# Moving gain multiplies, gate products and weight conversions between engines at the stage boundaries of a four-layer recurrent trunk

## The chip, the cores and the metric

The kernel runs on one core of a Trainium2 chip. The metric is the device time of one execution in microseconds (us); less is better. The engines are named as in the profile: PE (TensorE, matmuls) with its weight loads PEld, DVE (VectorE), ACT (ScalarE), POOL (GpSimd) and SP (SyncE, which issues the DMAs, in order).

## The reference

One inference step of a small trunk, in fp32: 1024 prompt positions and 8 x 8 sampled positions, model width 1024, FFN width 2816, 8 heads of 128.

```python
def conv_ffn(x, buf, w_in, cw, cb, w_out):
    gate, up = jnp.split(x @ w_in, 2, axis=-1)
    gc, new_buf = causal_dwconv(gate, buf, cw, cb)          # width 3, per column
    return (jax.nn.gelu(gc) * up) @ w_out, new_buf

for i in range(DEPTH):                                      # DEPTH = 2
    if i % 2 == 0:
        mix, h, cbuf = rglru_mixer(x, ...)                  # gated linear recurrence, 8 heads
    else:
        mix, S = hgrn2_mixer(x, ...)                        # below
    x = layer_norm(ALPHA * x + mix, ln_g[i, 0], ln_b[i, 0])
    f, fbuf = conv_ffn(x, ...)
    x = layer_norm(ALPHA * x + f, ln_g[i, 1], ln_b[i, 1])
```

`hgrn2_mixer` projects x to q, f, v and g, turns f into a forget gate, runs a chunked matrix-state recurrence per head, normalises the output `o` of each head and forms `o * silu(g)` before the output projection. The outputs are the new x, the recurrent states and the last rows of the convolutions.

## The kernel before, in words

The residual stream `z` stays on chip as nine row blocks m of 128 rows (the ninth has 64) by 1024 columns. Every matrix product is done in three reduced-precision products: each operand is split in a high and a low part (`xa`, `x` for activations, `wb`, `wx`, `wxf`, `wr` for weights), and the products are high*high, high*low, low*high. So three matmul lines always stand together: L298 to L300 (input projection of HGRN2), L606 to L608 (mixer output), L1144 to L1146 (FFN output).

**Weights.** A raw tile comes by DMA from SP's queue (L140, into `raw` or `rawf`). ACT casts the high part (L185 or L214), POOL subtracts it for the low part (L186 or L215) into one of three places `wb` and a few more. `convert` makes one tile if a place is free, `pump` issues loads and calls `convert`, `release` gives places back after a step. Which engine subtracts is in `run["lo"]`.

**FFN input.** `products` (L1045, tile `ps_f`) multiplies 2 x 2 blocks with seven products instead of eight. The weight combinations for them are made by POOL (L178, L180, L182), the activation combinations by `to_sums(mp)` for row blocks mp and mp + 4: PE transposes (L373), ACT copies (L393, L390), DVE and POOL adds (L391 to L400). `to_sums` uses parts of `z` as scratch. The product loops over i = 0..6, and for the first pair of columns over two column parts c outside of it.

**Layer norm.** `ln_pipeline` runs behind the matmuls that make a block: `resid` adds the product to z (L411), `nrm_a` takes the statistics (L421 on DVE, L422 to L424 on ACT), `nrm_b` scales (L429 to L434 on DVE, then the gain multiply L436 on POOL) and `nrm_c` adds the bias (L447 on DVE) and saves z to memory (L452). With `sums=True`, after each mixer, the blocks come in the order 8, 0, 4, 1, 5, 2, 6, 3, 7, and `to_sums` follows as pairs get done; what remains is put in `pend` and done within the next step's work.

**FFN output.** `prod` sums over the columns j of a group (six in the first) for one row block m and column half n in one PSUM bank (`ps_fo`). The operand of each j is split by `y_part` (ACT copy, DVE L1131). Banks come from a ring of four.

**HGRN2 recurrence.** Work of head h is cut into pieces that are run between the matmuls of projections. In a `period`, `gram` makes decayed Gram products by halving levels (L1394 on POOL, L1401 on ACT, L1404 on DVE, L1424 on PE, masked copies L1434), `kq_prep` and `pair_prep` scale keys and queries (L1472 to L1498), `gate_batch` applies the sigmoid to f and q of the next head and to g of the head before (L1334 to L1342), `g_mul` multiplies y by g (L1592), `f_chain_a` and `f_chain_b` make the logs and prefix sums of the next head's gate (L1351 to L1368), `gram_pairs` makes the last Gram level (L1451, masked copy L1452), `kt_small` transposes keys and makes `vb` (L1518 on POOL), `p_small` updates the state (L1532, L1538, L1543).

The tile pools add waits by data, so the order in which a function issues instructions is the order on each engine. Lines of the profile are those of the kernel before.

## Time and profile before

| | |
|---|---|
| median of 3 runs | 2645.24 us (2645.12 to 2646.01) |
| profiled execution | 2643.24 us, span 2641.5 us |
| granted TensorE clock, mean | 0.972 of full speed |
| PE busy | 2528.3 us, 96% of the span |
| DVE, ACT, POOL busy | 1566.3 (59%), 950.4 (36%), 1425.1 us (54%) |

The span is the time from the first to the last instruction; the rest of the execution lies around it. A row of the timeline has start, duration, engine, line, operation, output<-input and, in brackets, how long the engine sat idle before and what released it. Rows with `x4` are four instructions in a row. An instruction's duration includes the time that it waits for something below the level of semaphores, so the same product has different durations at different places.

### The profile page before, as it was taken

How to read it: one execution, taken by the hardware profiler on the slowest of the kernel's cores; microseconds unless marked ns; L12 is line 12 of the kernel's file. 1: busy time of each engine (PE TensorE's matmuls, PEld its weight loads, DVE VectorE, ACT ScalarE, POOL GpSimd, SP SyncE). 2: the span in 40 equal slices, each digit the busy share in tenths (PEclk: the TensorE clock that was granted, in tenths of full speed). 3: DMA queues.
4: the chain of work that ended last, by engine and by line, in shares of the span. 5: the costliest groups of instructions: out<-in, count | busy, mean ns of one | idle time of the engine just before them, and what ended most of it. 6: DMA issues, size and time to landing. Idle time of an engine off the chain costs nothing. (4 is left out here: it accounts for less than half of the span.)

```text
span 2641.5 us, 39929 instructions
## 1 busy us (share of the span) xinstructions
PE 2528.3 (96%) x16007; PEld 2332.4 (88%) x16007; DVE 1566.3 (59%) x2412; ACT 950.4 (36%) x1643; POOL 1425.1 (54%) x1169
## 2 busy tenths in 40 slices
PE   9999969999999999989999999999799999999997
PEld 9999869999998888779898988877699999988886
DVE  5986456565556333748858486875566565662327
ACT  4775233233334011334445353453333333330113
POOL 2443378888875112336445453635788888841214
PEclk9999989999999999999899999999899999999999
DMA  4115122222225322121111111123223222263111
GB/s 131 39 45 166 36 72 66 83 80 84 83 66 184 133 81 82 58 78 57 42 33 42 50 42 34 53 67 115 64 73 92 83 66 83 77 232 131 58 46 71
DMA packets 205840, 209.80 MB, mean 79 GB/s; under 512 B 13201, under 2 KB 167953, under 8 KB 205614
## 3 DMA queue, kind: packets, MB, share of 16 engines
q1 hardware_dynamic: 205654, 207.25, 24.4%
q8 instruction: 126, 2.06, 0.3%
q14 instruction: 60, 0.49, 0.1%
HBM read 159.61 MB, written 47.61 MB: 78 GB/s over the span
## 5 line engine op out<-in xcount | busy, mean ns | idle before, releaser
L215 POOL TENSOR_TENSOR wb<-raw,wb 128x1024 fp32r<-128x1024 f32 (+1 forms) x80 | 195.8, 2451 | 577.2 <-ACT wb L214 371.6
L1045 PE MATMUL ps_f<-xa,wb 128*128 128x288 f32 (+1 forms) x3072 | 406.9, 293 | 28.4 <-ACT wb L185 24.3
L1045 PEld LDWEIGHTS ps_f<-xa,wb 128*128 128x128 f32 x3072 | 398.9, 192 | 32.0 <-ACT wb L185 24.9
L1050 DVE TENSOR_TENSOR z<-z,ps_f 128x256 f32<-128x256 f32 (+2 forms) x550 | 196.2, 378 | 364.8 <-PE ps_f L1045 307.9
L1045 PE MATMUL ps_f<-x,wb 128*128 128x288 f32 (+1 forms) x2496 | 322.8, 289 | 0.0
L1045 PEld LDWEIGHTS ps_f<-x,wb 128*128 128x128 f32 x2496 | 318.1, 189 | 0.0
L298 PE MATMUL ps_in<-xa,wb 128*128 128x384 f32 (+3 forms) x912 | 307.4, 337 | 5.7 <-ACT wb L214 5.4
L300 PE MATMUL ps_in<-xa,wb 128*128 128x384 f32 (+3 forms) x912 | 300.5, 330 | 6.1 <-POOL wb L215 6.1
L299 PE MATMUL ps_in<-xa,wb 128*128 128x384 f32 (+3 forms) x912 | 300.6, 330 | 0.3 <-DVE xa L356 0.3
L411 DVE SCALAR_TENSOR_TENSOR z<-z,ps_fo 128x512 f32<-128x512 f32 x128 | 87.8, 686 | 285.8 <-PE ps_fo L1146 273.1
L186 POOL TENSOR_TENSOR wb<-rawf,wb 128x512 fp32r<-128x512 f32 x116 | 165.6, 1436 | 57.0 <-ACT wb L185 56.3
L186 POOL TENSOR_TENSOR wb<-raw,wb 128x512 fp32r<-128x512 f32 x116 | 160.5, 1391 | 58.3 <-ACT wb L185 48.8
L214 ACT CAST wb<-raw 128x1024 fp32r<-128x1024 f32 (+1 forms) x83 | 82.0, 987 | 301.4 <-issue 189.9
L1098 DVE SCALAR_TENSOR_TENSOR z<-z,ptf 128x1104 f32<-128x1104 f32 x88 | 182.0, 2069 | 1.6
L298 PEld LDWEIGHTS ps_in<-xa,wb 128*128 128x128 f32 x912 | 173.7, 190 | 8.4 <-ACT wb L214 5.7
L300 PEld LDWEIGHTS ps_in<-xa,wb 128*128 128x128 f32 x912 | 173.2, 190 | 7.5 <-POOL wb L215 6.8
L299 PEld LDWEIGHTS ps_in<-xa,wb 128*128 128x128 f32 x912 | 173.7, 190 | 1.4 <-DVE xa L356 0.7
L436 POOL TENSOR_TENSOR z<-z,gb 128x1024 f32<-128x1024 f32 (+2 forms) x36 | 101.6, 2822 | 107.7 <-DVE z L434 107.7
L1045 PE MATMUL ps_f<-xa,wxf 128*128 128x256 f32 (+1 forms) x1152 | 149.8, 288 | 0.1
L1045 PEld LDWEIGHTS ps_f<-xa,wxf 128*128 128x128 f32 x1152 | 146.6, 188 | 0.5 <-ACT z L1065 0.5
L185 ACT CAST wb<-rawf 128x512 fp32r<-128x512 f32 x116 | 71.0, 623 | 209.6 <-POOL rawf L182 76.0
L185 ACT CAST wb<-raw 128x512 fp32r<-128x512 f32 x116 | 70.2, 623 | 195.8 <-POOL raw L182 63.7
(493 smaller groups left out, 5816.7 us busy)
## 6 DMA issues: line engine op xcount, KB each, us to landing
raw<-in_ffn_w_in_dram SPq DMA_DIRECT2D x44, 512.0 KB
rawf<-in_ffn_w_in_dram SPq DMA_DIRECT2D x44, 512.0 KB
ysave<-z SPq DMA_DIRECT2D x44, 512.0 KB
raw<-in_hg_w_in_dram SPq DMA_DIRECT2D x32, 512.0 KB
xa<-ysave SPq DMA_DIRECT2D x28, 544.0 KB
zsave<-z SPq DMA_DIRECT2D x24, 512.0 KB
raw<-in_ffn_w_out_dram SPq DMA_DIRECT2D x24, 512.0 KB
z<-zsave SPq DMA_DIRECT2D x24, 512.0 KB
```

The costliest lines, as they stand in the source:

```text
L185: act.copy(w[:, 0], src)
L186: run["lo"].tensor_tensor(w[:, 1], src, w[:, 0], ALU.subtract)
L214: act.copy(w[:, 0, :n], raw[:, :n])
L215: run["lo"].tensor_tensor(w[:, 1, :n], raw[:, :n], w[:, 0, :n], ALU.subtract)
L298: pe.matmul(ps[:, :n], lhsT=wh, rhs=xh, start=(k == 0), stop=False)
L299: pe.matmul(ps[:, :n], lhsT=wh, rhs=xl, start=False, stop=False)
L300: pe.matmul(ps[:, :n], lhsT=wl, rhs=xh, start=False, stop=(k == KT - 1))
L411: dve.scalar_tensor_tensor(zz, zz, a, ps, ALU.mult, ALU.add, accum_out=stat[:, m, n:n + 1] if acc else None)
L436: eng.tensor_tensor(z[:r, m, c], z[:r, m, c], gb[:r, 0, c], ALU.mult)
L1045: pe.matmul(ps[:, :n], lhsT=l, rhs=r, start=(kk == 0 and i < 4 and l is wh and r is xh), stop=(kk == 3 and l is wl), skip_group_check=(i > ...
L1050: dve.tensor_tensor(d, s, pv(ps), ALU.add)
L1098: dve.scalar_tensor_tensor(c[:, :L], gs[:, i:i + L], w[:, i:i + 1], c[:, :L], ALU.mult, ALU.add)
```

## The change

Six edits:

1. In a norm with sums, the gain multiply of the last two row blocks (3 and 7) goes from POOL to DVE.
2. At the end of every norm but the last, the places of the weights that its matmuls used are released when the last matmuls have been issued, and `convert` is called before and after the last `nrm_b`. The low parts made there go to POOL after a mixer, and to DVE at the start of HGRN2 (three 128x1024 subtractions).
3. `to_sums(2)` runs within the norm instead of among the FFN's first products. `to_sums(3)` runs before product i = 5 instead of i = 4 of the first column part.
4. Pairs 0 to 3 of `to_sums` use blocks (0,4), (0,4), (1,8), (2,6) as scratch instead of their own.
5. In the first group of the FFN output, the products j = 0 to 3 of the first three row blocks run first, then j = 4 and 5 of each.
6. In the recurrence, the product of g with its sigmoid and the product of y with g go from POOL to DVE in the periods of heads 1 to 6; `vb` is made in a function of its own, ahead of these on POOL.

```diff
@@ def to_sums(mp)
-            s = [z[:, m, i * 512:(i + 1) * 512].rearrange("p (k t) -> p k t", t=n) for m in ms for i in range(2)]
+            s = [z[:, m, i * 512:(i + 1) * 512].rearrange("p (k t) -> p k t", t=n)
+                 for m in ((0, 4), (0, 4), (1, 8), (2, 6))[mp] for i in range(2)]
@@ def parts(m)
+        if m in run["dve"]:
+            return (dve, slice(0, D)),
         return (pool, slice(0, D)),
@@ def ln_pipeline(...)
+        run["dve"] = order[-2:] if sums else ()
...
             elif final != "out":
+                if i == NT:
+                    release(run["held"])
+                lo = run["lo"]
+                run["lo"] = pool if sums else dve
+                convert()
                 mid()
+                convert()
+                run["lo"] = lo
...
-            if final != "out" and 3 <= i < NT:
+            if final != "out" and 3 <= i < NT + sums:
                 turn(order[i - 3])
...
-            for m in order[NT - 3:]:
-                if not sums or m >= 4:
-                    pend.append(lambda m=m: turn(m))
+            for m in order[NT - 1 if sums else NT - 3:]:
+                pend.append(lambda m=m: turn(m))
@@ gates of the first pair
-                    fills = {(2, 0): [fill], (4, 0): [flush]}
+                    fills = {(5, 0): [flush]}
@@ first groups of the FFN output
+                        first = 3 if n == 0 and gi == 0 else 0
+                        banks = [sbank("ps_fo") for _ in range(first)]
+                        for m in range(first):
+                            prod_part(banks[m], m, grp, ws, range(4))
                         for m in range(NT):
-                            prod(m, n, grp, ws, gi == 0, False)
+                            if m < first:
+                                prod_part(banks[m], m, grp, ws, range(4, grp[1]))
+                                resid(m, n, banks[m], True)
+                            else:
+                                prod(m, n, grp, ws, gi == 0, False)
@@ def period(h)
-                fns.append(lambda: gate_batch([h + 1], [h - 1] if h else [], pool))
+                fns.append(lambda: vb_prep(h))
+                fns.append(lambda: gate_batch([h + 1], [h - 1] if h else []))
                 if h:
-                    fns.append(lambda: g_mul(h - 1, pool))
+                    fns.append(lambda: g_mul(h - 1))
```

`prod_part` is the loop over j of `prod` for a given range of j. Lines after an edit shift: L436 becomes L438, L447 L451, L391 L393, L394 L396, L429 to L434 L431 to L436, L1144 to L1146 become L1160 to L1162, L1045 L1057, L1342 L1366, L1592 L1618, L1336 L1360, L1452 L1476, L1518 L1544.

The first place is the end of a norm with sums, on DVE (`gb` holds gain and bias, `stat` the statistics, `ps_f` is the FFN product). Before:

```order
L434 TENSOR_SCALAR z<-z,stat 128x1024
L421 TENSOR_SCALAR stat<-stat 128x1
L447 TENSOR_TENSOR z<-z,gb 128x1024
L429 TENSOR_SCALAR stat<-stat 128x1
L430 SCALAR_TENSOR_TENSOR stat<-stat 128x1
L431 TENSOR_SCALAR stat<-stat 128x1
L432 TENSOR_TENSOR stat<-stat 128x1
L434 TENSOR_SCALAR z<-z,stat 128x1024
L447 TENSOR_TENSOR z<-z,gb 128x1024 x2
L1050 TENSOR_TENSOR z<-z,ps_f 128x256
```

And in the changed kernel, from the second L434 (now L436) on:

```order
L436 TENSOR_SCALAR z<-z,stat 128x1024
L438 TENSOR_TENSOR z<-z,gb 128x1024
L451 TENSOR_TENSOR z<-z,gb 128x1024
L396 TENSOR_TENSOR z<-ps_t,z 128x512
L397 TENSOR_TENSOR z<-z,ps_t 128x512
L393 TENSOR_TENSOR xa<-ps_t,xa 128x4x128
L399 TENSOR_TENSOR z<-ps_t,z 128x512
L402 TENSOR_TENSOR z<-ps_t,z 128x512
L393 TENSOR_TENSOR x_0_2500<-ps_t,x_0_2500 128x4x128
L393 TENSOR_TENSOR x_0_2504<-ps_t,x_0_2504 128x4x128
L451 TENSOR_TENSOR z<-z,gb 128x1024
L1062 TENSOR_TENSOR z<-z,ps_f 128x256
```

The gain multiply (L438) has come onto DVE, and a whole set of sums (L396 to L393) stands between the last two bias adds (L451).

The second place is PE at the end of the first tile of the FFN output, n = 0. Before, product j = 4 follows j = 3 and the next tile follows j = 5:

```order
L1144 MATMUL ps_fo<-wxf_2934,xa 128x512
L1145 MATMUL ps_fo<-wxf_2934,xa 128x512
L1146 MATMUL ps_fo<-wxf_2934,xa 128x512
L1144 MATMUL ps_fo<-wxf_2934,xa 128x512
L1145 MATMUL ps_fo<-wxf_2934,xa 128x512
L1146 MATMUL ps_fo<-wxf_2934,xa 128x512
L1144 MATMUL ps_fo<-wb_86,xa 128x512
```

In the changed kernel, from j = 3 of the first tile on:

```order
L1160 MATMUL ps_fo<-wb_84,xa 128x512
L1161 MATMUL ps_fo<-wb_84,xa 128x512
L1162 MATMUL ps_fo<-wb_84,xa 128x512
L1160 MATMUL ps_fo<-wb_86,xa 128x512
L1161 MATMUL ps_fo<-wb_86,xa 128x512
```

After j = 3 (weights `wb_84`) the next tile's j = 0 (`wb_86`) comes, and the products with `wxf` follow when three tiles have got that far.

The third place is DVE in a period of the recurrence, from `pair_prep` to the last masked copies (`A` is the Gram matrix, `mk` its mask, `y8h` holds y and g). Before:

```order
L1497 TENSOR_TENSOR z<-z 128x544
L1498 TENSOR_TENSOR z<-z,th_9712 128x544
L1336 TENSOR_TENSOR th_9711<-th_9711,z 128x1088
L1351 TENSOR_SCALAR z<-z,lbt 128x1088
L1352 TENSOR_SCALAR z<-z 128x1088
L1353 TENSOR_SCALAR z<-z 128x1088
L1357 TENSOR_SCALAR th_9712<-z 128x1088
L1358 TENSOR_SCALAR z<-z 128x1088
L1452 COPY_PREDICATED A<-mk,ps_g 128x4x128 x2
```

In the changed kernel:

```order
L1521 TENSOR_TENSOR z<-z 128x544
L1522 TENSOR_TENSOR z<-z,th_9718 128x544
L1360 TENSOR_TENSOR th_9717<-th_9717,z 128x1088
L1366 TENSOR_TENSOR y8h<-y8h,z 128x1088
L1618 TENSOR_TENSOR y8h<-y8h 128x1088
L1375 TENSOR_SCALAR th_9719<-th_9719,lbt 128x1088
L1376 TENSOR_SCALAR z<-th_9719 128x1088
L1377 TENSOR_SCALAR z<-th_9719 128x1088
L1381 TENSOR_SCALAR th_9718<-th_9719 128x1088
L1382 TENSOR_SCALAR th_9719<-th_9719 128x1088
L1476 COPY_PREDICATED A<-mk,ps_g 128x4x128 x2
```

The two gate products (L1366, L1618) stand ahead of the gate chain and of the masked copy.

More of the change, by code (lines that the diff above doesn't have):

```diff
@@ L106, in hawk_hgrn2_convffn_deepnorm_kernel @@
     steps = []
-    run = {"ch": CH, "dma": 0, "cvt": 0, "phase": -1, "n": 0, "lo": dve}
+    run = {"dve": (), "ch": CH, "dma": 0, "cvt": 0, "phase": -1, "n": 0, "lo": dve}
     blocks = []
@@ L263, in run_steps @@
                     assert convert(), "no place for weights"
-                fn([blocks[i].w[0] for i in ids])
                 held = run.setdefault("held", [])
                 held.extend(ids)
+                fn([blocks[i].w[0] for i in ids])
                 if not (keep and steps[run["n"] + 1][3]):
@@ L1133, in prod, with prod_part @@
         def prod(m, n, grp, ws, scaled, acc):
+            ps = sbank("ps_fo")
+            prod_part(ps, m, grp, ws, range(grp[1]))
+            resid(m, n, ps, scaled, acc)
+        def prod_part(ps, m, grp, ws, js):
             f0, nf, i0 = grp
-            ps = sbank("ps_fo")
-            for j in range(nf):
+            for j in js:
                 y = yv[i0 + j]
@@ L1150, in prod @@
                     pe.matmul(ps, lhsT=yt, rhs=wl, start=False, stop=b)
-            resid(m, n, ps, scaled, acc)
         def states(g):
@@ L1514, in kt_small, with vb_prep @@
         T.put(kd)
-        vb = T.get()
-        s["vb"] = vb
+    def vb_prep(h):
+        vb = G["T"].get()
+        hg[h]["vb"] = vb
         v8 = G["v"][:NS, NT - 1, (h % 2) * P:(h % 2 + 1) * P]
@@ L1734, in last_smalls @@
             run_all(lambda: gram(h, 5), *ysp(4)),
-            run_all(lambda: kt_small(h), lambda: rms_small(h - 1)),
+            run_all(lambda: kt_small(h), lambda: vb_prep(h), lambda: rms_small(h - 1)),
             run_all(lambda: pair(h), *ysp(5, 6)),
```

## The prediction

> **What bounds the kernel now.** I read four views: the page's head, TensorE's list of waits, the timeline of every engine around each long wait, and a table by stage for the granted clock. In a row of the list of waits stand: engine, tile, line, what it waited for: us in all, times, longest.
>
> ```profile
> PE 2528.3 (96%) x16007; PEld 2332.4 (88%) x16007; DVE 1566.3 (59%) x2412; ACT 950.4 (36%) x1643; POOL 1425.1 (54%) x1169
> PE ps_f L1045 <- ACT wb L185: 24.3, 2, 12.9
> PE ps_p L1532 <- DVE A L1452: 13.6, 6, 2.5
> PE ps_fo L1146 <- DVE xa L1131: 10.7, 4, 3.6
> PE ps_in L300 <- POOL wb L215: 6.1, 1, 6.1
> 1300.00:1730.00 430.00, 410.54 (x2657) 383.82 (x2656) 295.76 (x481) 182.50 (x286) 219.18 (x217) 0.94 0.15 43
> ```
>
> TensorE is busy for 2528.3 us of a span of 2641.5, so 113 us of idleness is nearly all that can be won, and the change adds or removes no matmul. The first four waits are 54.7 us of it, and each of them is a place that the change touches. The last row (start:end, length, busy us of PE, PEld, DVE, ACT and POOL, clock) adds a second prize: with a clock of 0.94, six heads of the recurrence lose about 0.06 x 430 = 26 us.
>
> **A. From a mixer's norm to the FFN (twice).**
>
> ```profile
> 352.30 1.22 DVE L447 TENSOR_TENSOR z<-z,gb 128x1024 f32<-128x1024 f32 x1
> 357.04 3.25 POOL L436 TENSOR_TENSOR z<-z,gb 128x1024 f32<-128x1024 f32 x1 [1.32 <-DVE z L434]
> 360.25 1.26 POOL L178 TENSOR_TENSOR raw<-raw 128x512 f32<-128x512 f32 x1
> 361.54 0.62 ACT L185 CAST wb<-raw 128x512 fp32r<-128x512 f32 x1 [7.32 <-POOL raw L178]
> 362.21 0.85 PE L1045 MATMUL ps_f<-xa,wb 128*128 128x288 f32 x2 [12.93 <-ACT wb L185]
> 363.03 1.44 SPq L140 DMA_DIRECT2D rawf<-in_ffn_w_in_dram  x2
> 369.34 0.69 DVE L394 TENSOR_TENSOR z<-ps_t,z 128x512 f32<-128x512 f32 x1 [1.72 <-ACT z L393]
> 375.39 0.69 DVE L391 TENSOR_TENSOR x<-ps_t,x 128x512 fp32r<-128x512 f32 x1 [0.31 <-ACT x L390]
> 379.85 0.60 ACT L393 COPY z<-ps_t 128x512 f32<-128x512 f32 x1
> 382.56 1.74 PE L1045 MATMUL ps_f<-xa,wb 128*128 128x256 f32 x4 [0.34 <-ACT xa L390]
> ```
>
> TensorE waits 12.93 us for the second weight tile of the FFN. Its preparation, POOL L178, stands behind POOL's gain multiply L436 of the last row block. The change moves the last two of these multiplies to VectorE and lets the conversions go ahead of them. A 128x1024 product takes VectorE 1.22 us by L447, so two cost 2.4 us there and free about 6.6 us on POOL; the weight is then ready near 356. But other things are late next. The sums of blocks 2 and 6 are now made inside the norm; by the rows at 369.34 and 375.39 one set takes 376.08 - 369.34 = 6.74 us of VectorE. On VectorE the gain multiply of block 3 starts where the first L447 stands now, at 352.30; adding the multiplies, both adds L447 and the small statistics, VectorE is free near 360.6 and done with the sums at 367.3. Only then comes the last add, until 368.5. SP's queue is in order: its zsave waits for that add, and the next rawf load, issued at 363.03 now, stands behind it and goes out near 368.7. Landing takes at most 5.7 us (rows in C), so ACT can convert it at 374.4; the last transposed sums (ACT L393) follow in ACT's queue, and from there the second column part starts 382.56 - 379.85 = 2.7 us later. With the conversion ahead and POOL's share I get 378.6 instead of 382.56: 4.0 us saved, not 12.9. The second boundary has the same rows 1509 us later. A = 2 x 4.0 = 8 us. Lower end 1 each (the load 3 us later still); upper end 12.93 - 6.74 = 6.2 each, where nothing but the sums replaces the wait.
>
> **B. First output tiles of the FFN (twice).**
>
> ```profile
> 2348.42 0.39 PE L1144 MATMUL ps_fo<-wb,xa 128*128 128x512 f32 x1
> 2356.53 0.79 PE L1146 MATMUL ps_fo<-wxf,xa 128*128 128x512 f32 x1 [3.56 <-DVE xa L1131]
> 2359.98 0.79 PE L1146 MATMUL ps_fo<-wxf,xa 128*128 128x512 f32 x1 [1.80 <-DVE xa L1131]
> 2353.12 6.94 DVE L1131 TENSOR_TENSOR xa<-xa 128x1024 fp32r<-128x1024 f32 x4
> 2369.50 0.69 DVE L411 SCALAR_TENSOR_TENSOR z<-z,ps_fo 128x512 f32<-128x512 f32 x1 [6.08 <-DMA z<-zsave]
> 2375.33 0.69 DVE L411 SCALAR_TENSOR_TENSOR z<-z,ps_fo 128x512 f32<-128x512 f32 x1
> 2379.52 0.69 DVE L411 SCALAR_TENSOR_TENSOR z<-z,ps_fo 128x512 f32<-128x512 f32 x1 [2.23 <-PE ps_fo L1146]
> ```
>
> The product j of a tile needs its split operand, which VectorE makes (L1131); j = 4 and 5 come late, at 2356.5 and 2360. The change runs j = 0 to 3 of three tiles first: 36 matmuls instead of 12 from 2348.42 on. Two whole tiles of 18 matmuls are read 2379.52 - 2375.33 = 4.19 us apart, 0.233 each, so TensorE works until 2356.8. It still waits 2.0 us for j = 5 at 2359.98, finishes the three tiles at 2363.0 and the fourth at 2367.2. Then four PSUM banks hold unread tiles. The first is read by L411 at 2369.50, after a reload of z that is queued behind other DMAs and does not depend on TensorE; so a new wait of 3.0 us arises, to 2370.2. The fifth tile ends at 2374.4, against 2379.4 now (L411 at 2379.52 waits for it): 5.0 us. After a wait of this length I allow 1.1 us for half clock (an estimate: five matmuls at twice 0.23). B = 2 x 3.9 = 8 us; ends 0 (all given back at the bank) and 5 each.
>
> **C. Start of the HGRN2 projection (once).**
>
> ```profile
> 1128.25 1.06 ACT L214 CAST wb<-raw 128x1024 fp32r<-128x1024 f32 x1
> 1129.36 0.79 PE L298 MATMUL ps_in<-xa,wb 128*128 128x512 f32 x1 [5.45 <-ACT wb L214]
> 1131.04 3.25 POOL L436 TENSOR_TENSOR z<-z,gb 128x1024 f32<-128x1024 f32 x1 [3.91 <-DVE z L434]
> 1136.64 0.79 PE L300 MATMUL ps_in<-xa,wb 128*128 128x512 f32 x1 [6.06 <-POOL wb L215]
> L215 DVE TENSOR_TENSOR wb<-raw,wb 128x1024 fp32r<-128x1024 f32 x3 | 3.7, 1219 | 0.2 <-ACT wb L214 0.2
> 1138.11 9.63 SPq L140 DMA_DIRECT2D raw<-in_hg_w_in_dram  x3
> 1143.80 1.05 ACT L214 CAST wb<-raw 128x1024 fp32r<-128x1024 f32 x1
> ```
>
> The first wait stays: the conversion L214 does not move. The second goes: the low part L215 stood behind L436 on POOL; on VectorE it takes 1.22 us, right after ACT at 1129.31, so L300 can start at 1130.6, when the two matmuls before it end. C = 6.06 - 0.1 = 6 us. The last POOL multiply starts some 1.2 us later, and ACT's third conversion now stands ahead of the first evacuation and waits for a load (1138.11 to 1143.80 at most, here issued near 1131); TensorE has 24 matmuls of the next tile to cover that. Ends 4.5 and 6.1.
>
> **D. The recurrence.** In six heads the two gate products (L1342, L1592) move from POOL to VectorE, ahead of the masked copy L1452 for which TensorE waits; L1518 runs earlier on POOL.
>
> ```profile
> 1379.19 2.82 POOL L215 TENSOR_TENSOR wb<-raw,wb 128x1024 fp32r<-128x1024 f32 x1
> 1381.98 2.94 POOL L1518 TENSOR_TENSOR z<-v,sm 64x1024 f32<-64x1024 f32 x1
> 1371.75 1.27 DVE L1482 TENSOR_TENSOR z<-z 128x1088 f32<-128x1088 f32 x1
> 1374.13 2.69 DVE L1497 TENSOR_TENSOR z<-z 128x544 f32<-128x544 f32 x1
> 1379.73 3.43 DVE L1336 TENSOR_TENSOR th<-th,z 128x1088 f32<-128x1088 f32 x1
> 1388.21 1.34 DVE L1452 COPY_PREDICATED A<-mk,ps_g 128x512 f32<-128x512 int32 x2
> 1388.99 1.16 PE L1532 MATMUL ps_p<-v,z 128*128 128x128 f32 x8 [2.14 <-DVE A L1452]
> 1437.60 0.70 DVE L1498 TENSOR_TENSOR th<-th,z 128x544 f32<-128x544 f32 x1
> 1453.19 3.45 PE L1543 MATMUL ps_p<-z 64*128 64x512 f32 x4
> 1458.19 0.58 PE L1630 MATMUL ps_v<-wb,xa 128*128 128x256 f32 x1 [0.50 <-DVE gb L1538]
> ```
>
> A 128x1088 product takes VectorE 1.27 us with POOL idle, and L1336 of the same size takes 3.43 beside POOL L215: it ends 1.2 us after the POOL instruction ends (1382.01, then 1383.16). L1497, half the size, takes 2.69 instead of about 0.70. So VectorE sits through four POOL instructions in turn before L1452: L1342, L1592, L215, L1518. The Trainium skill, page "SBUF — State Buffer", section "Who interferes with whom", says why: VectorE and GpSimd share a pair of ports under an exclusive lock, and a VectorE instruction with two SBUF inputs blocks against a GpSimd instruction that reads SBUF. The rows agree, and by that rule a removed POOL product gives its time back to VectorE where it stood in the way, which would give the same sum.
>
> I walk VectorE's queue through the period at 1374 to 1389, in which it has no idle time. The low parts L215 held the port from 1379.8 to 1382.0, 2.2 us; L1518 from 1383.16 to 1384.92, 1.8; from there L1351 to L1358 took 3.3 until L1452. After the change L1518 runs some 17 us earlier, beside four L1404, and I charge its 1.8 there. So L1452 starts at 1374.1 + 1.8 + 1.4 (L1497, L1498) + 2.2 (L215, once) + 3.6 (three products) + 3.3 = 1386.4, not 1388.21: 1.8 us earlier, and TensorE's wait of 2.14 shrinks to 0.3. Six times 1.8 is D = 11 us. The lower end is 12 x 1.27 = 15 us lost (products added, nothing given back). The upper end is 13.6 + 26 = 39 us, with the waits gone and the clock full throughout.
>
> I count nothing for the clock. L1543 takes 3.45 us after the wait at 1452 where full speed would take about half, so the wait does cost clock. But when TensorE comes sooner it meets the next link, L1630 behind DVE L1538, which moves by only 1.8 us; the idle time moves there. The Trainium skill, page "TensorE: Matmul & The Clock Gate", Part 1, has the clock fall after about 3.4 us of idling. By that alone these 2.2 us waits would cost no clock; the row at 1453 speaks against it.
>
> **Sum.** 8 + 8 + 6 + 11 = 33 us. The profiled execution took 2643.24 us (span 2641.5 and 1.7 around it): 2610. The median of the runs is 2645.24, 2.0 higher: 2612. About 0.2% (5.3 us) can be told from no change.
>
> **Rivals.**
> - Clock won too: with the 2.2 us waits gone, the half-clock stretches of the recurrence go. For: the stretches follow those waits. Against: L1538. Half of 26 us and the rest of the 13.6: D = 28, total 50, 2595.
> - Late loads and full banks: A and B give 1 each per place and D half. For: SP's order in A, the bank in B. 2 + 2 + 6 + 6 = 16: 2629.
> - Slower: every moved product meets a POOL instruction and takes 3.43 us like L1336, and VectorE's neighbours stay as slow. L1452 comes 2 x 3.43 = 6.9 us later in six periods, 41 us, less A, B, C (22): 2645 + 19 = 2664. It decides from 4.6 us a period (22 + 5.3 over six). Against: two of the four POOL instructions in the way are the ones removed.
> - No change: VectorE comes 3 to 4 us later per period and eats A, B, C: 2645.
>
> **How the numbers follow.** Forecast 0.47, clock won 0.20, late loads 0.19, no change 0.07, slower 0.07. So faster 0.86, same 0.07, slower 0.07. The likeliest is 2612. The range runs from 2590 (clock won, a little more) to 2634 (late loads with D at nothing is 2635); it leaves out about 2 in 10, above for the most part.
>
> **What would show it.** A: the wait of 12.93 becomes several below 4, the second column part starts near 378.6, the rawf load near 368.7. B: the waits for L1131 become one of about 2 us, and a new one of 3 us for PSUM behind L411 appears. C: no wait at L300. D: L1336 and the products near 1.2 us except one in each period, waits for the masked copy of 0.3 us. The prediction is wrong if those waits grow instead, if the clock from 1300 to 1730 leaves 0.94 by 0.02 or more, or if TensorE waits longer for weights after the norms.

## The result and the profile after

The changed kernel takes 2615.36 us (median of 4 runs, 2611.44 to 2616.62) against 2645.18 us of the kernel before on the same chip: a ratio of 0.9884, 95% interval 0.9867 to 0.9902, so about 30 us less. The profiled execution took 2615.03 us, its span 2613.3. The head of the page and rows from the list of TensorE's waits after the change (engine, tile, line, what it waited for: us in all, times, longest):

```profile
PE 2506.9 (96%) x16007; PEld 2317.7 (89%) x16007; DVE 1559.5 (60%) x2431; ACT 951.9 (36%) x1643; POOL 1378.8 (53%) x1150
PE ps_t L373 <- DVE z L451: 22.3, 4, 9.0
PE ps_v L1656 <- DVE gb L1564: 7.3, 3, 2.4
PE ps_f L1057 <- ACT z L395: 6.8, 2, 3.4
PE ps_kt L1536 <- DVE A L1464: 5.7, 7, 1.4
...
PE ps_fo L1160 <- DVE z L413: 4.1, 2, 3.0
...
PE ps_fo L1162 <- DVE xa L1143: 3.9, 2, 2.0
```

The four waits that led the list before are gone or smaller, and others stand in their places. The number of matmuls is the same, 16007. The span is 28.2 us shorter; 21.4 of that is TensorE's busy time (2528.3 to 2506.9) and only 6.8 is idle time. The same matmuls were done in less time: they ran at a higher clock. Where that shortens the kernel is to be read by stage. Of the 21.4 us, 13.1 lie in stage D of the table below, 6.8 in the two stages A, 2.5 in B and C, and the start has 1.0 more. In A the idle time grew (21.0 to 21.6 and 19.7 to 22.4 us), and the nine runs below that share A's code take 516.9 to 517.1 us for the first and 515.9 to 516.2 for the second, with 8.5 to 13.7 us lost to the clock: there another chain sets the length, and the clock does not. In D the length follows the clock, and that is the main reading of this case.

The stages are cut at landmarks on TensorE (the first L373 of the first mixer's norm, the first output product of each FFN, the first product of HGRN2's input, the first ps_g of the recurrence, the first L373 of the second mixer's norm, the last matmul). Their lengths, in us of the two profiles:

| stage | before | after | change | forecast |
|---|---|---|---|---|
| start, to the first norm's sums | 320.66 | 322.51 | +1.85 | 0 |
| A, first | 518.80 | 516.97 | -1.83 | -4.0 |
| B, first | 289.90 | 285.08 | -4.82 | -3.9 |
| C | 62.44 | 56.13 | -6.31 | -6.0 |
| D | 638.98 | 625.24 | -13.74 | -11 |
| A, second | 517.64 | 516.01 | -1.63 | -4.0 |
| B, second | 279.09 | 277.36 | -1.73 | -3.9 |

The start is not an effect of the change: in this execution the clock was halved from 11.8 to 15.2 us, in a part whose instructions are the same; runs below with the same start (e5, e1) stand at 320.7 there. Below stands stage D in one row each (start:end, length, busy us of PE, PEld, DVE, ACT, POOL, clock, DMA share, GB/s), of before, of after, and the row of after that answers to the last row of the prediction's first list:

```profile
1191.80:1830.78 638.98, 613.58 (x3793) 561.46 (x3793) 453.16 (x763) 277.26 (x446) 314.78 (x297) 0.95 0.18 53
...
1180.69:1805.93 625.24, 600.49 (x3793) 553.86 (x3793) 433.08 (x775) 277.80 (x446) 284.85 (x285) 0.98 0.18 54
1300.00:1730.00 430.00, 410.96 (x2704) 385.01 (x2703) 294.08 (x506) 195.33 (x305) 189.09 (x199) 0.97 0.15 42
```

Both have 3793 matmuls. TensorE's idle time in D is 25.4 us before (638.98 - 613.58) and 24.8 after; its busy time fell by 13.1. Summing (1 - clock) x length over 40 equal pieces of D gives 28.9 us lost to the clock before and 15.5 after. So the clock's 13.4 us are all of D but 0.3.

### The profile page after: what moved, and what is told of

Same layout as the page of the kernel before. It is cut to its first block, busy times and chain, and to the rows that moved or that the text cites. A ratio compares the mean times of both kernels' runs of the same rounds, so it can differ in the third digit from the quotient of the medians.

```text
span 2613.3 us, 39952 instructions
## 1 busy us (share of the span) xinstructions
PE 2506.9 (96%) x16007; PEld 2317.7 (89%) x16007; DVE 1559.5 (60%) x2431; ACT 951.9 (36%) x1643; POOL 1378.8 (53%) x1150
## 5 line engine op out<-in xcount | busy, mean ns | idle before, releaser
L215 POOL TENSOR_TENSOR wb<-raw,wb 128x1024 fp32r<-128x1024 f32 (+1 forms) x77 | 201.2, 2616 | 618.4 <-ACT wb L214 415.7
L1057 PE MATMUL ps_f<-xa,wb 128*128 128x288 f32 (+1 forms) x3072 | 399.7, 290 | 15.0 <-ACT z L395 6.8
L1057 PEld LDWEIGHTS ps_f<-xa,wb 128*128 128x128 f32 x3072 | 392.5, 189 | 18.1 <-ACT z L395 7.6
L1057 PE MATMUL ps_f<-x,wb 128*128 128x288 f32 (+1 forms) x2496 | 323.0, 289 | 2.4 <-POOL wb L186 1.3
L1057 PEld LDWEIGHTS ps_f<-x,wb 128*128 128x128 f32 x2496 | 318.1, 189 | 3.2 <-POOL wb L186 1.7
L300 PE MATMUL ps_in<-xa,wb 128*128 128x384 f32 (+3 forms) x912 | 299.7, 329 | 0.0
L413 DVE SCALAR_TENSOR_TENSOR z<-z,ps_fo 128x512 f32<-128x512 f32 x128 | 87.8, 686 | 279.0 <-PE ps_fo L1162 266.5
L300 PEld LDWEIGHTS ps_in<-xa,wb 128*128 128x128 f32 x912 | 172.4, 189 | 1.4 <-DVE wb L215 0.8
L1057 PE MATMUL ps_f<-xa,wxf 128*128 128x256 f32 (+1 forms) x1152 | 149.8, 288 | 2.7 <-ACT z L1077 2.7
L1057 PEld LDWEIGHTS ps_f<-xa,wxf 128*128 128x128 f32 x1152 | 146.6, 189 | 3.1 <-ACT z L1077 3.1
L438 POOL TENSOR_TENSOR z<-z,gb 128x1024 f32<-128x1024 f32 (+2 forms) x32 | 88.6, 2767 | 103.4 <-DVE z L436 103.4
```

The source lines that it names most:

```text
L215: run["lo"].tensor_tensor(w[:, 1, :n], raw[:, :n], w[:, 0, :n], ALU.subtract)
L300: pe.matmul(ps[:, :n], lhsT=wl, rhs=xh, start=False, stop=(k == KT - 1))
L413: dve.scalar_tensor_tensor(zz, zz, a, ps, ALU.mult, ALU.add, accum_out=stat[:, m, n:n + 1] if acc else None)
L438: eng.tensor_tensor(z[:r, m, c], z[:r, m, c], gb[:r, 0, c], ALU.mult)
L1057: pe.matmul(ps[:, :n], lhsT=l, rhs=r, start=(kk == 0 and i < 4 and l is wh and r is xh), stop=(kk == 3 and l is wl), skip_group_check=(i > ...
```

## The experiments

Every run is on a chip with the kernel before beside it (medians of 2645.2 to 2646.7 us), and each edit is against the changed kernel unless said otherwise. One table for all, with the stages as above (the second A and B after the bar); "clock" is the us lost to the clock in D, worked out as above.

| run | median (range) us | ratio, 95% | A | B | C | D | clock | A / B second |
|---|---|---|---|---|---|---|---|---|
| e1 products on POOL | 2626.08 (2625.11-2632.97) | 0.9929 (0.9915-0.9944) | 516.95 | 285.15 | 56.31 | 638.46 | 29.1 | 515.96 / 275.89 |
| e2 whole tiles | 2621.59 (2619.62-2622.67) | 0.9907 (0.9890-0.9923) | 517.10 | 289.27 | 57.29 | 623.60 | 13.7 | 515.96 / 279.59 |
| e3 low parts on POOL | 2612.98 (2611.71-2617.90) | 0.9878 (0.9863-0.9892) | 517.10 | 285.18 | 58.55 | 623.76 | 13.7 | 515.95 / 274.40 |
| e4 gain on POOL | 2617.56 (2616.39-2618.44) | 0.9891 (0.9877-0.9906) | 518.90 | 285.24 | 56.54 | 625.85 | 17.2 | 517.52 / 274.43 |
| e5 products late | 2604.45 (2603.53-2606.24) | 0.9841 (0.9826-0.9856) | 516.90 | 285.13 | 56.02 | 618.54 | 10.4 | 515.98 / 277.25 |
| e6 vb late | 2613.07 (2612.28-2615.72) | 0.9875 (0.9857-0.9894) | 516.93 | 285.25 | 57.46 | 623.05 | 13.7 | 515.97 / 275.99 |
| e7 sums later | 2613.61 (2612.90-2614.51) | 0.9875 (0.9860-0.9890) | 518.12 | 285.31 | 56.83 | 623.21 | 13.7 | 517.20 / 274.42 |
| e8 two tiles | 2615.28 (2614.47-2616.07) | 0.9881 (0.9866-0.9896) | 516.93 | 286.96 | 57.26 | 623.57 | 13.7 | 516.05 / 276.76 |
| e9 filled waits | 2605.75 (2602.95-2607.79) | 0.9844 (0.9830-0.9857) | 516.92 | 285.13 | 57.51 | 617.33 | 6.8 | 515.98 / 274.80 |
| e10 all late | 2599.74 (2597.70-2600.19) | 0.9821 (0.9807-0.9834) | 516.88 | 285.22 | 56.01 | 612.36 | 6.7 | 516.18 / 274.46 |
| e11 no refill | 2625.02 (2623.87-2625.14) | 0.9914 (0.9900-0.9927) | 520.48 | 285.10 | 62.81 | 625.62 | 15.5 | 519.01 / 274.46 |
| e12 all late, own blocks | 2602.46 (2601.33-2605.38) | 0.9832 (0.9819-0.9845) | 516.96 | 285.15 | 56.47 | 615.25 | 6.8 | 515.95 / 275.71 |

### e1: the gate products back on POOL

```diff
-                fns.append(lambda: vb_prep(h))
-                fns.append(lambda: gate_batch([h + 1], [h - 1] if h else []))
+                fns.append(lambda: gate_batch([h + 1], [h - 1] if h else [], pool))
                 if h:
-                    fns.append(lambda: g_mul(h - 1))
+                    fns.append(lambda: g_mul(h - 1, pool))
...
@@ vb is made at the end of kt_small(h), as in e6 below
```

> Undoes the recurrence's part of the change alone: both gate products go back to POOL and vb is made in kt_small again. By landmarks of the two traces the recurrence is 13.7 us shorter after the change. Theory (VectorE's line to the masked copy got 1.8 us shorter per period, and with it the half-clock stretches): all of the 13.7 us comes back, about 2629 us; the six waits for the masked copy are back at 2.2 us each and the clock of the stage falls to 0.94. Rival (the clock gain is a matter of where the stage happens to start, not of the products): the waits come back but the clock stays near 0.97, about 2616 to 2620 us.

D in this run's windows, and one of its six waits for the masked copy:

```profile
1179.05:1817.51 638.46, 612.85 (x3793) 560.38 (x3793) 452.62 (x763) 276.81 (x446) 313.51 (x297) 0.95 0.17 53
...
1376.16 1.16 PE L1556 MATMUL ps_p<-v,z 128*128 128x128 f32 x8 [2.15 <-DVE A L1476]
```

D is back at 638.5 with the waits for the masked copy, and at the old clock: 25.6 us idle, 612.9 busy. So edit 6 is what makes D, and it makes it by the clock. The median gave back 10.7 us, less than D's 13.2: in this profile the start and the second B are 1.9 and 1.5 us shorter than in the changed kernel's.

### e6: vb late again, products on DVE

```diff
-                fns.append(lambda: vb_prep(h))
@@ def kt_small(h), at its end
+        vb = T.get()
+        s["vb"] = vb
+        pool.tensor_tensor(vb..., v8..., G["sm"]..., ALU.mult)
```

> The products stay on VectorE where the change puts them, but vb is made in kt_small again, behind the weight conversion. Theory (the early vb blocks four L1428 and delays VectorE by 1.8 us, as the prediction charged it, and that is what TensorE waits for at L1536): the 1.0 to 1.4 us waits at L1536 go, but vb then blocks the gate chain for the same 1.8 us, so the stage stays within 3 us, 2613 to 2618 us. Rival (the early vb is what made the gain): most of the 13 us of the recurrence is lost, 2625 us or more.

The median lies 2.3 us from the changed kernel's, and D is 623.1: the earlier `vb` is not what made the gain. As the theory has it, the waits at L1536 go and waits for the masked copy of up to 1.6 us stand in their place.

### e5: the products behind what TensorE waits for

For heads 1 to 4 the sigmoid of g goes into a free block of `y8`, and both products are issued at the end of the period, behind `p_small`.

```diff
-                fns.append(lambda: gate_batch([h + 1], [h - 1] if h else []))
-                if h:
+                fns.append(lambda: gate_batch([h + 1], [h - 1] if h else [], spare=y8[:, h + 3] if 1 <= h <= 4 else None))
+                if h > 4:
                     fns.append(lambda: g_mul(h - 1))
@@ end of period(h), odd heads; even heads alike
-            p.append(run_all(lambda: o_small(h), lambda: prep(h + 1, 1)))
+            p.append(run_all(lambda: o_small(h), lambda: prep(h + 1, 1), lambda: products_late(h)))
...
@@ products_late(h) issues both products of heads 1 to 4
```

> The two gate products stay on VectorE, but in four of the six periods (heads 1 to 4) they stand behind the state update and the next head's first scalings instead of ahead of the gate chain and the masked copy. Theory (VectorE's line from L1360 to the state update L1564 sets when TensorE can go on, and the idle time there costs clock): that line gets 1.2 + 3.3 = 4.5 us shorter in each of the four, the 2.4 us waits at L1656 of heads 1 and 3 go and with them their half clock; 2 x (2.4 + 3.4) in odd heads and about 2 x 0.6 in even ones, 8 to 13 us faster than the changed kernel, 2603 to 2607 us. Rival (TensorE is now the bound and the clock falls for other reasons): under 3 us gained, 2612 us or more.

The first product of the value projection, in head 1 (late) and head 5 (not late):

```profile
1285.14 0.39 PE L1661 MATMUL ps_v<-wb,xa 128*128 128x256 f32 x1 [0.28 <-DVE gb L1569]
...
1580.18 0.58 PE L1661 MATMUL ps_v<-wb,xa 128*128 128x256 f32 x1 [2.44 <-DVE gb L1569]
```

Where the products are late, the wait of 2.4 us is 0.3; where they are not, it stands as in the changed kernel. The median is 10.9 us lower, as the theory has it. The two profiles are 8.8 us apart; D gives 6.7 of that, and the start, which the edit does not touch, 1.85.

### e9: work in TensorE's waits

```diff
-    def turn_odd():
+    def turn_odd(times=1):
...
-        for i in range(4):
-            pe.transpose(ps[:, i * P:(i + 1) * P], G["A"][:, 2 * i + 1], ident)
+        for i in range(4 * times):
+            pe.transpose(ps[:, i % 4 * P:(i % 4 + 1) * P], G["A"][:, 2 * (i % 4) + 1], ident)
...
-            turn_odd()
+            turn_odd(5 if h in (1, 3, 5) else 1)
```

> The changed kernel with one addition: in heads 1, 3 and 5 the four transposes of turn_odd (L1485, 0.66 us a group, 0.11 us each) are issued five times over into the same place with the same result, so that TensorE works for about 1.8 us of the 2.42 us in which it waits at L1656 (1287.3 to 1289.7, 1437.1 to 1439.6, 1587.1 to 1589.5). Nothing that another engine does comes later but the copy of ps_at (used 8 us on). Theory: each of these waits is followed by 6.8 us at half clock (the granted clock reads 0.50 from 1288.5 to 1295.0), a loss of 3.4 us each, and it is TensorE's idleness that brings it; filled, the waits keep their end and the half clock goes or shrinks to one piece of 3.4 us: the recurrence, 625.2 us in the changed kernel's profile and 623 to 626 in its kin, falls by 5 to 10 us, total 2605 to 2610. Rival: the fall of the clock has another cause (a phase of the program, the other engines, chance), or it lies beside other work: the time stays at 2612 to 2616, and the clock shows the same three stretches of 6.8 us.

Head 1's wait in the changed kernel, with the clock in the wait, in the 6.8 us behind its fall, and after that; the last row has the 6.8 us from the end of the wait on:

```profile
1289.70 0.58 PE L1656 MATMUL ps_v<-wb,xa 128*128 128x256 f32 x1 [2.42 <-DVE gb L1564]
...
1287.10:1288.50 1.40, 0.17 (x2) 0.00 (x0) 1.39 (x6) 0.59 (x1) 0.52 (x1) 0.95 0.00 0
1288.50:1295.30 6.80, 5.60 (x26) 5.60 (x27) 6.49 (x17) 1.99 (x2) 4.64 (x6) 0.51 0.00 0
1295.30:1300.00 4.70, 4.70 (x43) 4.70 (x42) 2.24 (x3) 0.33 (x1) 2.74 (x4) 1.00 0.78 215
1289.70:1296.50 6.80, 6.80 (x37) 6.80 (x38) 6.65 (x15) 1.99 (x2) 4.64 (x6) 0.60 0.03 6
```

The same place with the wait filled:

```profile
1288.54 2.40 PE L1485 MATMUL ps_at<-ident,A 128*128 128x128 f32 x20
1291.63 0.39 PE L1656 MATMUL ps_v<-wb,xa 128*128 128x256 f32 x1 [0.69 <-DVE gb L1564]
...
1288.50:1291.60 3.10, 2.44 (x21) 2.17 (x20) 2.97 (x10) 0.59 (x1) 1.68 (x3) 1.00 0.00 0
1291.60:1298.40 6.80, 6.77 (x59) 6.77 (x60) 6.61 (x15) 2.00 (x2) 4.63 (x5) 1.00 0.03 7
1182.09:1799.42 617.33, 598.61 (x3842) 552.62 (x3841) 443.14 (x775) 277.32 (x446) 284.52 (x285) 0.99 0.18 55
```

In the 6.8 us behind the wait, 59 matmul records begin or run, at clock 1.00, where it was 37 at 0.60. Nothing was taken away and 48 matmuls were added, and the median is 9.6 us lower; in the profiles D gives 7.9 of it. This shows by itself that at these three places TensorE's idleness brings the half clock, and that the half clock, not the wait, is what they cost.

### e10 and e12: all gate products late

```diff
@@ both: products_late(h) acts for every head but 0, and no g_mul is left in the middle of period(h)
...
@@ e10, against e5
-spare=y8[:, h + 3] if 1 <= h <= 4 else None
+spare=y8[:, 7] if h else None
@@ e12, against e5
+spare=y8[:, h + 3 if h < 5 else h] if h else None
@@ e12, end of period(5) and of period(6); the other heads as in e5
+            run_all(lambda: products_late(h), lambda: o_small(h), lambda: prep(h + 1, 1))
+            run_all(lambda: products_late(h), lambda: pair_recip(h + 1), lambda: prep(h + 1, 1))
```

> The kernel with the two gate products placed after the p-products (2604.45 us), with head 5's and head 6's products placed late as well (the sigmoid kept in the last block of y8, free until head 7). Theory: what head 5's place in the queue still costs is one wait of 2.44 us at the value projection (the row at 1580.18) and the 3.4 us lost in the half clock behind it: 3 to 6 us less, 2599 to 2602, with no wait over 2 us at the value projection's first product in the recurrence. Rival: the wait is only moved behind the products, or another wait (the masked copy's, 1.35 us) takes its place with the same clock loss: 2603 to 2606.

> All gate products late: as the run with heads 5 and 6 late too (2599.74 us), but with head 5's and head 6's sigmoids kept in the block of y8 that is their own and free until then, and the products of these two heads just behind the p-products, ahead of the output products. Theory: only the place of these two heads' products differs by some us in VectorE's queue, behind the additions that free the value projection's banks, so the 2.44 us wait stays gone: 2597 to 2603. Rival: before head 5's output evacuation the products (2.5 us) hold back the banks of ps_o or the next head's exponents, and 2 to 4 us come back: 2602 to 2606.

In e10 the block is not free: it holds head 5's gate by then, so some heads are multiplied by other values; only the order and the places of its instructions are read here. It took 2599.74 us, by the theory. e12 computes the gates as they are and is the fastest full kernel of the study: 2602.46 us, 12.9 below the changed kernel, of which D gives 10.0 in the profiles. That time lies in the range of its theory and in the range of its rival, so it does not choose between them. Head 5's wait in e12:

```profile
1590.22 0.38 PE L1661 MATMUL ps_v<-wb,xa 128*128 128x256 f32 x1 [0.25 <-DVE y8h L1610]
```

The 2.4 us are gone, and what the 0.25 us still wait for is the output of the heads (L1610). D loses 6.7 to 6.8 us to the clock in both. e12's lies 2.9 us above e10's D; that products ahead of `o_small` cost this, as the rival has it, was not tried apart.

### e2 and e8: how many output tiles go in two parts

```diff
-                        first = 3 if n == 0 and gi == 0 else 0
+                        first = 0        # e2; e8 has 2 in place of 3
```

> Undoes the split of the first output tiles alone. By landmarks the two places gained 4.8 and 1.7 us. Theory (the split fills the wait for the split operands until the PSUM ring is full): 6.6 us come back, about 2622 us, with 3.6 and 1.8 us waits for L1143 at both places. Rival (the reload of z ends both orders at the same time): no change, 2615 us.

> Two tiles instead of three are run in two parts. Theory (the end of the place is set by the reload of z that frees the first PSUM bank, since with three tiles TensorE then waits 1.2 and 3.0 us for it): the new wait goes, the one for L1143 grows, and the time stays within 1.5 us, 2614 to 2617 us. Rival (each tile ahead is worth a third of the 6.2 us): 2 us slower, 2617.5 us or more.

e2 gives 6.2 us back, in B: edit 5 is worth about 6. With two tiles (e8) the waits for the split operand are 1.94 and 2.48 us and the wait for a bank behind L413 is gone:

```profile
2335.20 0.79 PE L1162 MATMUL ps_fo<-wxf,xa 128*128 128x512 f32 x1 [2.48 <-DVE xa L1143]
```

The medians of e8 and of the changed kernel are equal within 0.1 us, in the range of e8's theory. But in the profile the first B of e8 is 1.9 us longer, while the eleven profiles with three tiles there have 285.1 to 285.3 with 0.9 to 3.4 us lost to the clock. In e8 6.8 us of half clock begin between its two waits, and TensorE then reaches the bank too late to wait for it. So whether two tiles are worth as much as three is not settled by one total.

### e3: the low parts at HGRN2's start on POOL, at the new place

```diff
-                run["lo"] = pool if sums else dve
+                run["lo"] = pool
```

> Leaves the three low parts at the start of HGRN2 on POOL, but where the change issues them, ahead of the last gain multiply. Theory (it was the place in POOL's queue that held L300, not POOL's speed): L215 runs right behind ACT's cast and takes 2.4 us instead of 1.2, so about 1.2 us come back, 2616.6 us. Rival (the engine matters, as the prediction had it): 4 to 6 us come back, 2619 to 2621 us.

```profile
1127.51 0.79 PE L300 MATMUL ps_in<-xa,wb 128*128 128x512 f32 x1 [1.21 <-POOL wb L215]
```

With POOL making the low part, the wait is 1.2 us, not 6.06. It was mostly the place behind the gain multiply in POOL's queue that cost; POOL's slower subtraction costs the remaining 1.2 us. The total, forecast at 2616.6 and measured at 2612.98, does not show these 1.2 us.

### e4, e7, e11: what makes A

```diff
@@ e4
-        run["dve"] = order[-2:] if sums else ()
+        run["dve"] = ()
@@ e7
-            if final != "out" and 3 <= i < NT + sums:
+            if final != "out" and 3 <= i < NT:
...
-                    fills = {(5, 0): [flush]}
+                    fills = {(2, 0): [fill], (5, 0): [flush]}
@@ e11: the release, both convert() and the lines with lo and run["lo"] around mid() are left out
```

> Leaves the gain multiply of the last two row blocks on POOL, all other edits kept. Theory (beside POOL's conversions VectorE's multiplies cost 2.2 us, not 1.2, so moving them won little): the boundaries change by less than 2 us each, 2612 to 2619 us. Rival (the move is what lets the conversions go ahead): POOL holds the conversions again, 4 us and more lost at each boundary, 2623 us or above.

> to_sums(2) goes back behind the norm, ahead of product i = 2, all other edits kept. Theory (with the sums inside, their transposes wait 9.0 us in front of the FFN's first products, which had all they need): TensorE runs 24 matmuls in that wait, VectorE does the last add and its save first, the rawf load goes out some 7 us sooner; 1 to 4 us faster at each boundary, 2607 to 2613 us. Rival (the sums are the long chain, and any delay of them comes out at the end): 2 us slower at each boundary, 2619 us.

> The changed kernel without the release and the two conversions within the last three turns of the layer norms (edit 2 undone at all three boundaries; the gain multiplies, the later sums and the rest stay). Theory: at the two starts of the FFN the conversions on GpSimd that stand beside the last gain multiplies and bias adds (VectorE 2.16 to 2.31 us instead of 1.22) go, so that VectorE is through with the sums' inputs some 3 us earlier; but the wait for the first weights (12.9 us before, on the ACT conversion) comes back, 5 to 13 us long, in place of the 9.0 and the 3.4 us: 2 to 6 us later at each start. At the recurrence's start the low part's wait at L300 comes back (6.1 us before), about 5 us. Total 2624 to 2632. Rival: the early conversions do not pay at the FFN's starts, since their collision with VectorE costs as much as the weights' wait: only the 5 us at the recurrence come back, 2618 to 2622.

In e7 the later sums read blocks that others have used as scratch by then, so their values differ; only the order is tested.

Each of the three parts alone, taken back, makes A longer: without the gain multiplies on DVE by 1.9 and 1.5 us, which is all that A had won; with the sums later by 1.2 each; without the early release and conversions (e11) by 3.5 and 3.0. Together that is more than A had won, so each rests on the others. e4's theory held (2617.56, each boundary within 2 us). e7's theory, 1 to 4 us faster per boundary, fell: its total is 1.8 us lower only because D and the last B, with the same instructions, are 2.0 and 2.9 us shorter in its profile. e11's theory held (2625.02, in its range), and its rows show a collision of VectorE and POOL that was left out of the prediction. The first A in the changed kernel, engine by engine:

```profile
357.49 1.97 PE L373 MATMUL ps_t<-ident,z 128*128 128x128 f32 x8 [8.99 <-DVE z L451]
353.07 1.00 DVE L434 TENSOR_TENSOR stat<-stat 128x1 f32<-128x1 f32 x1
358.82 1.73 DVE L436 TENSOR_SCALAR z<-z,stat 128x1024 f32<-128x1024 f32 x1
360.58 2.16 DVE L438 TENSOR_TENSOR z<-z,gb 128x1024 f32<-128x1024 f32 x1
362.67 2.29 DVE L451 TENSOR_TENSOR z<-z,gb 128x1024 f32<-128x1024 f32 x1
371.53 2.31 DVE L451 TENSOR_TENSOR z<-z,gb 128x1024 f32<-128x1024 f32 x1
358.73 1.27 POOL L186 TENSOR_TENSOR wb<-raw,wb 128x512 fp32r<-128x512 f32 x1 [4.67 <-ACT wb L185]
359.95 1.71 POOL L180 TENSOR_TENSOR raw<-raw,raw 128x512 f32<-128x512 f32 x1
362.39 1.48 POOL L186 TENSOR_TENSOR wb<-raw,wb 128x512 fp32r<-128x512 f32 x1 [0.73 <-ACT wb L185]
371.43 1.33 POOL L393 TENSOR_TENSOR x<-z,x 128x512 fp32r<-128x512 f32 x1
374.28 1.45 SPq L140 DMA_DIRECT2D rawf<-in_ffn_w_in_dram  x2
378.98 0.62 ACT L185 CAST wxf<-rawf 128x512 fp32r<-128x512 f32 x1 [0.51 <-DMA rawf<-in_ffn_w_in_dram]
382.56 0.39 PE L1057 MATMUL ps_f<-xa,wb 128*128 128x256 f32 x1 [0.98 <-ACT xa L392]
```

And in e11, without conversions beside them (its last bias add, at 367.01, meets the subtraction of the sums on POOL, L393, as in the changed kernel):

```profile
358.09 1.22 DVE L438 TENSOR_TENSOR z<-z,gb 128x1024 f32<-128x1024 f32 x1
359.23 1.22 DVE L451 TENSOR_TENSOR z<-z,gb 128x1024 f32<-128x1024 f32 x1
367.01 2.27 DVE L451 TENSOR_TENSOR z<-z,gb 128x1024 f32<-128x1024 f32 x1
369.73 1.45 SPq L140 DMA_DIRECT2D rawf<-in_ffn_w_in_dram  x2
371.11 0.85 PE L1050 MATMUL ps_f<-xa,wb 128*128 128x288 f32 x2 [4.97 <-ACT wb L185]
...
1134.65 0.79 PE L300 MATMUL ps_in<-xa,wb 128*128 128x512 f32 x1 [6.06 <-POOL wb L215]
```

The gain multiply and the add behind it take 1.22 us there, and the rawf load goes out 47.9 us after the first sums (369.73 less the start of 321.79) against 51.8 in the changed kernel. But the weights come late again (4.97 us), and so does the low part at HGRN2's start (6.06).

## Why the prediction was right, and where not

The total, 2612 forecast and 2615.36 measured, is right. Its four terms sum to 33; the stages give 30.1, less the 1.85 of the start. A and B were too large, C has the right size with half of its cause, and D came near only because a gain by the clock, which it counted as nothing, stands in for a gain in idle time that did not come; that its number came out is luck.

**A, 8 forecast, 3.5 measured: the term was mis-sized.** The mechanism is as forecast: no wait of 12.93 us for the second weight tile, the sums and the rawf load late in its place. The step that failed is the timing of VectorE's queue. It put the moved gain multiply and the bias adds at 1.22 us, from the row at 352.30. In that row VectorE began 0.04 us ahead of POOL; the last add of the same norm, which began just behind POOL's L178 (the prediction's row at 360.25), already took 2.27:

```profile
352.34 3.37 POOL L436 TENSOR_TENSOR z<-z,gb 128x1024 f32<-128x1024 f32 x1 [1.33 <-DVE z L434]
360.32 2.27 DVE L447 TENSOR_TENSOR z<-z,gb 128x1024 f32<-128x1024 f32 x1 [2.23 <-POOL z L436]
```

The change puts POOL's conversions ahead of these products. The gain multiply took 2.16 us, the add behind it 2.29, L436 1.73 instead of 0.81 and the small L434 1.00 instead of 0.16: 3.8 us in all. Without these conversions, in e11, the load went out 47.9 us after the first sums, and 48.0 were forecast; in the changed kernel it was 51.8. (That e11 meets the forecast so closely is two misses that cancel: the sums begin 1.4 us sooner than forecast and the last add takes 1.1 longer.) The second column part started 60.05 us after the first sums against 61.90 before and 57.9 forecast. The wait did not become "several below 4" either, and TensorE's idle time in A did not shrink: one wait is 8.99 us, since the transposes of blocks 2 and 6 now stand ahead of the FFN's first products on TensorE and wait for block 6's bias add.

**B, 8 forecast, 6.6 measured: the half clock was mis-sized.** The waits came as forecast, 1.97 us for the split operand and 2.98 for the bank:

```profile
851.16 0.56 PE L1162 MATMUL ps_fo<-wxf,xa 128*128 128x512 f32 x1 [1.97 <-DVE xa L1143]
861.37 0.50 PE L1160 MATMUL ps_fo<-wb,xa 128*128 128x512 f32 x1 [1.17 <-DVE z L413]
...
2333.62 0.50 PE L1162 MATMUL ps_fo<-wxf,xa 128*128 128x512 f32 x1 [1.98 <-DVE xa L1143]
2344.10 0.80 PE L1160 MATMUL ps_fo<-wb,xa 128*128 128x512 f32 x1 [2.98 <-DVE z L413]
2344.00:2351.00 7.00, 6.90 (x18) 5.45 (x19) 6.92 (x12) 0.00 (x0) 0.00 (x0) 0.58 0.99 383
```

In the first, the half clock fell behind the first wait and was over before the bank came free, so it cost nothing and all 4.8 us were won. In the second it came behind the last wait and lasted 6.8 us, 3.4 lost where 1.1 were allowed. It is also a matter of the execution. Runs whose instructions there are the same take 274.4 to 274.8 us for this stage with no half clock (e3, e9, e10). With one piece of 3.4 us behind the first wait they take 274.4 too (e4, e7, e11), and the wait for the bank then shrinks from 2.7 us and more to 1.2. With one piece behind the bank's wait they take 275.7 to 276.0 (e12, e1, e6), and with two 277.3 (e5, the changed kernel).

**C, 6 forecast, 6.3 measured: the size right, the cause half wrong.** The first wait stayed and L300's is gone:

```profile
1124.56 0.80 PE L298 MATMUL ps_in<-xa,wb 128*128 128x512 f32 x1 [5.46 <-ACT wb L214]
```

The prediction gave the gain to VectorE's 1.22 us; e3 shows that the place alone gives most of it, since with POOL at the new place 1.21 of the 6.06 us are left.

**D, 11 forecast, 13.7 measured: the path on VectorE right, the account wrong.**

```profile
1362.07 0.75 DVE L1521 TENSOR_TENSOR z<-z 128x544 f32<-128x544 f32 x1
...
1364.57 1.28 DVE L1366 TENSOR_TENSOR y8h<-y8h,z 128x1088 f32<-128x1088 f32 x1
1365.88 3.34 DVE L1618 TENSOR_TENSOR y8h<-y8h 128x1088 f32<-128x1088 f32 x1
...
1372.70 1.35 DVE L1476 COPY_PREDICATED A<-mk,ps_g 128x512 f32<-128x512 int32 x2
```

From `pair_prep`'s first product to the masked copy VectorE takes 10.63 us, here and in three more of the six periods (10.62 and 10.18 in the others); the walk through its queue gave 10.5 (1386.4 less 1374.1 and the 1.8 charged earlier), and before it was 14.08. Two products take 1.28 us and one 3.34 beside POOL's L215, as said. The waits for the masked copy (13.6 us) are gone from the list. But the prediction then booked six shorter waits as the gain and counted nothing for the clock; that is the step that failed. The reason it gave, that the idle time moves to the value projection's first product, is what happened (7.3 us at L1656, and 5.7 more at the key transposes, L1536; idle time 25.4 and 24.8), and it should have brought the idle gain to nothing. What does not move along is the clock: 28.9 us were lost in D and 15.5 are. The loss comes in steps of 1.71 us (last section). Of the 17 steps before, 13 stand behind waits for the masked copy; of the 9 after, 6 stand behind the three waits at L1656. So 12 of the 13.4 us go with the waits. The other 4 and 3 steps stand behind small products, with 0.6 us of idleness or less ahead of them. By the rule the prediction set itself, a clock from 1300 to 1730 that leaves 0.94 by 0.02 or more counts against it, and it is 0.97. The rival with the clock won had the cause (26 us lost before, half of it won), and 13.4 is half of 26; it went wrong in adding the idle time (28 in all; its own terms, 13 and 13.6, add up to 26.6).

The Trainium skill, page "TensorE: Matmul & The Clock Gate", Part 1, gives one idle window of about 3.4 us as what makes the clock fall, and calls the window free-running. The pieces of half clock here are 3.41 us and whole multiples of it, which agrees; that a wait of 3.4 us is needed does not, since waits of 2.42 and 1.97 us did it.

## What to carry to other kernels

Before moving a wait, price the clock behind it: here waits of 2 to 2.5 us in the recurrence cost more by the half clock after them than by themselves, and useless work in such a wait was worth most of what removing it was (7.9 us of stage D in e9, 10.0 in e12). Where an instruction is moved to VectorE, look at what POOL will have begun by then: the same multiply and add took 1.22 us where VectorE began first and 2.16 to 2.31 where a short POOL instruction had. And place work that nobody waits for behind the chain that frees another engine's buffers: the same two products, moved from ahead of it to behind it, gave 10 us of D and 12.9 of the median.

## What the runs showed of the hardware

The granted clock changes only at fixed times. With windows of 0.25 us, all 18 stretches of half clock in the profile before, and all 14 in the profile after up to 2350 us, begin and end on a grid of 3.413 us that runs through from the first to the last, whatever TensorE does (in the profile after 1288.37 to 1295.19, 1387.36 to 1390.77, 2343.09 to 2349.91, each a whole number of 3.413 apart within 0.02 us). Each step costs up to 1.71 us; D lost 17 steps before and 9 after (29.0 and 15.4 us by the clock's own records), and the same stage in kernels that share its code differs by whole steps (the clock column: 13.7, 15.5, 17.2).

In the grid step just ahead of a fall, TensorE was idle for 1.1 us or more in most cases. In the profiles before, after and of e9, every step in full clock with more than 1.97 us of idleness was followed by a fall; with 1.0 to 1.97 us some were and some not (2.14 us of waiting at 1386.8 in the profile before, of which 1.85 fell into one step, brought none).

Ten of the 43 falls in these profiles had 0.7 us of idleness or less ahead, five of them 0.1 or none. In all ten the step holds the 16 products of 8 columns at the end of `o_small` (L1573 before, L1599 after), which take 1.95 us of it. Whether a fall follows goes by their place on the grid. In the profiles before, after, of e5, e9 and e12 there are 40 such groups. All 19 that begin between 0.09 and 0.45 of a step, and so end with it or before, are followed by a fall at its end; of the 21 others, earlier, later or across two steps, none is. The four steps that e9 and e12 still lose in D are all of this kind. So a measure of the work done in a step, not idleness alone, seems to decide; its threshold is not settled here, and other shapes of these small products were not tried.

VectorE and POOL hold each other up by who begins first. In the profiles before, after and of e11, a gain multiply or bias add of 128x1024 on VectorE took 1.21 to 1.23 us where it ran alone or began ahead of POOL's gain multiply, which then ended 2.2 to 2.3 us behind it. Wherever a TENSOR_TENSOR instruction of POOL had begun first, VectorE's ended 1.08 or 1.09 us behind the end of POOL's.
